# Where the halves of RWKV's token mixes are made: all of them on VectorE, stored split, and two LoRA products in float32

## The chip, the cores and the metric

One core of a Trainium2 chip runs the whole program. The metric is the device time of one launch in microseconds. The kernel before took 3241.56 us (median of three runs, 3240.18 to 3243.27). In the profile and below, PE is TensorE (PEld its weight loads), DVE is VectorE, ACT is ScalarE, POOL is GpSimd, and SP is SyncE, whose in-order queue issues nearly all DMAs.

## The reference

Two blocks follow one another on an activation of 256 tokens by 2048 features, in float32. The first block has four layers: an RWKV-7 mixer, a dilated attention, a pooling mixer, and again an RWKV-7 mixer. The second block has one attention with a linear recurrence and one mLSTM layer. The change touches only the front of the two RWKV mixers, which compute:

```
xx = shift(h) - h
r, k, v, g = [(h + xx * mu[j]) @ w_in[j] for j in 0..3]      # 2048 x 2048 each
xw, xa = h + xx * mu[4], h + xx * mu[5]
decay from tanh(xw @ w1) @ w2      (w1: 2048 x 96)
a     from (xa @ a1) @ a2          (a1: 2048 x 96)
v1, v2: the same kind of LoRA on the v mix, in the second RWKV layer only
```

After that come the recurrence over time (done in chunks of 64 tokens), a group norm, a gate with g, and the projection w_out (2048 x 2048).

## The kernel before

**Projections.** Every large product is made in three passes of the single-pass type float32r. Each operand is split into a high half (a cast, `split`, line 220, on ACT) and a low half (operand minus high half, line 221, on DVE), and TensorE adds high x high, high x low and low x high (line 262). `proj` runs over 512 columns of a weight at a time: over four chunks `c` of 512 input features and over two pairs of 128-row tiles, it loads 512 KB of weight into `wr` (3 buffers), splits it into `wh` and `wl` (5 buffers each, one k-tile each), and issues 6 matmuls per k-tile (3 passes for each of two token halves). The activation halves of a chunk are `ah` and `al`, four buffers each, so that one projection's input fills all of them.

**Order.** The code is written as generators (tasks) that a planner interleaves by estimated times; a scheduler then sets the final order of each engine's instructions when the program is built. Every engine works through its own list strictly in order.

**RWKV layer.** The mixes `h + xx*mu` are needed feature-major in chunks. `order` runs k, r, v for the first half of the columns and then again k, r, v for the second half, and the four column groups of g come last. So each mix is needed twice (g's only once, but late), and is kept in DRAM (`kept`, the `mix` tensors) in between:

- `first_mix` makes the k mix, chunk by chunk, at the layer's start; `mix` makes r and v while the projection before runs. The mix itself is one `scalar_tensor_tensor` on DVE per 128 features (line 485), then the split, then a DMA of the unsplit mix to DRAM (lines 517 and 498).
- `keep_g` makes the g mix by the slow way of `mixed`: a scaled copy on ACT (line 483) and an addition on POOL (line 487), and stores it unsplit (line 527).
- `again` reads a stored mix into an `st` buffer (2 buffers, 256 KB each, line 534) and splits it once more into `ah` and `al`.
- `lora` makes the w and a mixes by the slow way, casts the high half on ACT (line 576), subtracts on POOL (line 577), splits the LoRA weight into `z` buffers, and issues 12 float32r matmuls per chunk (`lora_mm`, lines 554 to 556).

**The blocks.** From the third projection on, `rwkv_blocks` runs eight blocks of the recurrence beside the projections: chains of small matmuls, DVE, ACT and POOL steps that carry high priority. From there until most of `w_out` is done, `lo_share = 3` sends every third weight's low half (line 221) to POOL in place of DVE.

Of the kernel before, what the change touches and what calls it, by code (L numbers as in the profile page):

```python
# [11 lines left out]
F32 = mybir.dt.float32  # L12
FR = mybir.dt.float32r
I32 = mybir.dt.int32
AF = mybir.ActivationFunctionType
OP = mybir.AluOpType
# [98 lines left out]
class Builder:  # L115
# [357 lines left out]
    def rwkv(self, ia, li):  # L473
# [4 lines left out]
        def mixed(m, j, c, a, slow=False):  # L478
            for f in range(2):
                ft = a * 2 + f  # L480
                mu = self.v("a_mu", ia * 6 + j, 16, c * 4 + ft)
                if slow:
                    nc.scalar.activation(m[:, f], st.xx[c][:, ft], AF.Copy, scale=mu)  # L483
                else:
                    ins = nc.vector.scalar_tensor_tensor(m[:, f], st.xx[c][:, ft], mu, st.h[c][:, ft], OP.mult, OP.add)  # L485
            if slow:
                ins = nc.gpsimd.tensor_tensor(m, m, st.h[c][:, a * 2:a * 2 + 2], OP.add)  # L487
            return ins

        kept = [self.dram.tile([128, 16, 256], F32, name="mix%d_%d" % (ia, j)) for j in range(4)]  # L490

        def mix(j, box, c):
            hi, lo = self.act_pair()
            for a in range(2):
# [3 lines left out]
                nc.sync.dma_start(kept[j][:, c * 4 + a * 2:c * 4 + a * 2 + 2], m)  # L498
# [3 lines left out]
        def first_mix(j, box):  # L502
# [5 lines left out]
            for u in range(8):  # L508
# [8 lines left out]
                nc.sync.dma_start(kept[j][:, c * 4 + a * 2:c * 4 + a * 2 + 2], m)  # L517
                if a:
                    box[c] = pair
                yield 0.6  # L520

        def keep_g():
            for c in range(4):
                for a in range(2):
                    m = self.t("st", [128, 2, 256], F32, 2)
                    mixed(m, 3, c, a, True)
                    nc.sync.dma_start(kept[3][:, c * 4 + a * 2:c * 4 + a * 2 + 2], m)
                    yield 3.0

        def again(j, box, c):  # L530
            hi, lo = self.act_pair()
            for a in range(2):
                m = self.t("st", [128, 2, 256], F32, 2)
                nc.sync.dma_start(m, kept[j][:, c * 4 + a * 2:c * 4 + a * 2 + 2])
                self.split(hi[:, a * 2:a * 2 + 2], lo[:, a * 2:a * 2 + 2], m)
# [31 lines left out]
        def lora(j, w1, n, tag, func):  # L567
            ws = lora_w(w1, n)
            q = self.gm()[0:n, 0:256]
            for c in range(4):  # L570
                hl = self.t("GM", [128, 2, 4, 256], FR, 3)
                for a in range(2):
                    m = self.t("e2", [128, 2, 256], F32, 7)
                    mixed(m, j, c, a, True)
                    s = slice(a * 2, a * 2 + 2)
                    nc.scalar.copy(hl[:, 0, s], m)
# [1281 lines left out]
```

## Time and profile before

| What | Value |
|---|---|
| median of three runs | 3241.56 us |
| profiled execution | 3250.24 us, with a span of 3247.1 us from first to last instruction |
| mean granted TensorE clock | 0.967 |
| PE, DVE, ACT, POOL busy | 93%, 71%, 55%, 24% of the span |
| HBM read and written | 527.88 MB and 46.15 MB, 177 GB/s over the span |

The profiled execution is 8.7 us longer than the median of the runs, and its span covers all but 3.1 us of it. The page gives busy shares over the whole span; the two RWKV layers fill about the first 800 us and the stretch from 1620 to 2410 us, and only there does the change move anything. A group's mean duration on DVE tells more than its busy time here, because the same instruction can take quite different times in different stretches.

### The profile page before, as it was taken

How to read it: one execution, taken by the hardware profiler on the slowest of the kernel's cores; microseconds unless marked ns; L12 is line 12 of the kernel's file. 1: busy time of each engine (PE TensorE's matmuls, PEld its weight loads, DVE VectorE, ACT ScalarE, POOL GpSimd, SP SyncE). 2: the span in 40 equal slices, each digit the busy share in tenths (PEclk: the TensorE clock that was granted, in tenths of full speed). 3: DMA queues.
4: the chain of work that ended last, by engine and by line, in shares of the span. 5: the costliest groups of instructions: out<-in, count | busy, mean ns of one | idle time of the engine just before them, and what ended most of it. 6: DMA issues, size and time to landing. Idle time of an engine off the chain costs nothing. (4 is left out here: it accounts for less than half of the span.)

```text
span 3247.1 us, 48857 instructions
## 1 busy us (share of the span) xinstructions
PE 3034.3 (93%) x17128; PEld 2452.2 (76%) x17128; DVE 2304.0 (71%) x4623; ACT 1783.2 (55%) x3504; POOL 794.6 (24%) x614
## 2 busy tenths in 40 slices
PE   6889999998999999999978898998989999999998
PEld 4667677776888888888856776777777788888886
DVE  7778778765666666676597788788557775666765
ACT  4565555444555555655555565554456765555554
POOL 4433443440112111020054325434312110000101
PEclk9999999999999999999989998999999999999999
DMA  5654453366666656666656644533665566666665
GB/s 186 200 193 145 155 175 121 122 200 203 178 174 178 177 169 205 205 211 191 208 174 219 197 152 153 171 119 105 206 214 160 156 188 203 182 199 172 186 187 169
DMA packets 327014, 577.24 MB, mean 178 GB/s; under 512 B 33856, under 2 KB 60776, under 8 KB 326768
## 3 DMA queue, kind: packets, MB, share of 16 engines
q1 hardware_dynamic: 326768, 574.12, 57.4%
q8 instruction: 134, 2.20, 0.3%
q14 instruction: 112, 0.92, 0.1%
HBM read 527.88 MB, written 46.15 MB: 177 GB/s over the span
## 5 line engine op out<-in xcount | busy, mean ns | idle before, releaser
L221 DVE TENSOR_TENSOR wl<-wr,wh 128x512 fp32r<-128x512 f32 x1580 | 1179.0, 758 | 690.8 <-ACT wh L220 664.3
L220 ACT CAST wh<-wr 128x512 fp32r<-128x512 f32 x1728 | 1052.4, 620 | 976.2 <-PE qps L262 452.9
L262 PE MATMUL qps<-wl,ah 128*128 128x512 f32 x3424 | 1385.8, 405 | 39.1 <-DVE wl L221 38.2
L262 PE MATMUL qps<-wh,al 128*128 128x512 f32 x3424 | 1368.7, 400 | 1.3 <-DVE al L221 1.3
L262 PE MATMUL qps<-wh,ah 128*128 128x512 f32 x3424 | 1266.3, 405 | 45.7 <-ACT wh L220 13.2
L262 PEld LDWEIGHTS qps<-wh,ah 128*128 128x128 f32 x3424 | 656.5, 192 | 191.0 <-ACT st L596 15.4
L262 PEld LDWEIGHTS qps<-wl,ah 128*128 128x128 f32 x3424 | 659.0, 192 | 187.2 <-DVE wl L221 53.3
L262 PEld LDWEIGHTS qps<-wh,al 128*128 128x128 f32 x3424 | 657.5, 192 | 137.9 <-DVE al L221 2.7
L221 POOL TENSOR_TENSOR wl<-wr,wh 128x512 fp32r<-128x512 f32 x148 | 203.6, 1385 | 363.9 <-ACT wh L220 336.3
L1103 POOL TENSOR_TENSOR q<-q,gain 128x1024 f32<-128x1024 f32 (+1 forms) x15 | 35.0, 2332 | 376.5 <-ACT sq L1097 376.5
L321 POOL TENSOR_TENSOR rstd<-rs_v,mhalf 128x2 f32<-128x2 f32 x7 | 5.0, 708 | 430.6 <-DVE rs_v L319 430.5
L277 PE MATMUL qtp<-cst,q 128*128 128x128 f32 x388 | 62.0, 289 | 23.0 <-DVE al L295 6.8
L838 PE MATMUL qtp<-q,q 64*128 64x128 f32 x512 | 72.4, 306 | 7.5 <-DVE GM L841 3.8
L277 PEld LDWEIGHTS qtp<-cst,q 128*128 128x128 f32 x388 | 48.5, 148 | 36.5 <-issue 20.5
L485 DVE SCALAR_TENSOR_TENSOR e<-q,vec,q 128x256 f32<-128x256 f32 x96 | 73.7, 811 | 0.0
L872 DVE TENSOR_TENSOR mb<-mb,Xc 128x120 f32<-128x120 f32 (+14 forms) x240 | 73.1, 305 | 0.1
L838 PEld LDWEIGHTS qtp<-q,q 64*128 64x128 f32 x512 | 57.9, 201 | 18.3 <-POOL q L811 5.1
L221 DVE TENSOR_TENSOR al<-st,ah 128x512 fp32r<-128x512 f32 x64 | 54.7, 871 | 23.5 <-ACT ah L220 23.4
L856 ACT COPY Md<-GM 32x128 f32<-32x128 f32 x128 | 55.3, 432 | 27.7 <-DVE GM L841 26.4
L220 ACT CAST ah<-st 128x512 fp32r<-128x512 f32 x64 | 38.3, 617 | 57.6 <-DMA st<-mix 49.7
L875 DVE TENSOR_TENSOR Xc<-Xc,mb 128x8 f32<-128x8 f32 x240 | 59.2, 247 | 1.1
L487 POOL TENSOR_TENSOR e<-e,q 128x512 f32<-128x512 f32 x32 | 48.2, 1521 | 31.8 <-ACT e L483 27.0
(388 smaller groups left out, 3383.2 us busy)
## 6 DMA issues: line engine op xcount, KB each, us to landing
wr<-a_w_in SPq DMA_DIRECT2D x256, 512.0 KB
wr<-b_w_in SPq DMA_DIRECT2D x160, 512.0 KB
wr<-odd_w_in SPq DMA_DIRECT2D x128, 512.0 KB
wr<-even_w_in SPq DMA_DIRECT2D x72, 512.0 KB
wr<-a_w_out SPq DMA_DIRECT2D x64, 512.0 KB
wr<-c_w_in SPq DMA_DIRECT2D x64, 512.0 KB
st<-mix SPq DMA_DIRECT2D x64, 256.0 KB
wr<-c_w_out SPq DMA_DIRECT2D x32, 512.0 KB
```

Of the source, the lines that this page charges most:

```text
L220: self.nc.scalar.copy(hi, src)
L221: (eng or self.nc.vector).tensor_tensor(lo, src, hi.bitcast(F32), OP.subtract)
L262: nc.tensor.matmul(o[:, cs], u[:, kk, sl], v[k][:, cs], start=st and x == 0 and c1 == 0, stop=sp and x == 2, skip_group_check=True)
L277: nc.tensor.transpose(q[:, f, t * 128:t * 128 + 128], src[:, t, (fp * 2 + f) * 128:(fp * 2 + f) * 128 + 128], self.ident)
L321: nc.gpsimd.tensor_tensor(r, v, self.mhalf[:, 0:2], OP.pow)
L485: ins = nc.vector.scalar_tensor_tensor(m[:, f], st.xx[c][:, ft], mu, st.h[c][:, ft], OP.mult, OP.add)
L487: ins = nc.gpsimd.tensor_tensor(m, m, st.h[c][:, a * 2:a * 2 + 2], OP.add)
L838: nc.tensor.matmul(qs[hp][:, c], BK[rs, f, c], AR[rs, f, c], start=True, stop=True)
L856: nc.scalar.copy(Md[rs, :, us].rearrange("p c u -> p u c"), GM2[rs, us, (1 - i // 2) ^ f, rs])
L872: nc.vector.tensor_tensor(mb[:, 0:n], mb[:, 0:n], Xc[:, r:r + 1].to_broadcast([128, n, 8]), OP.mult)
L875: nc.vector.tensor_tensor(Xc[:, r + 1], Xc[:, r + 1], mb[:, 0], OP.add)
L1103: nc.gpsimd.tensor_tensor(e3, e3, gain.unsqueeze(1).to_broadcast([128, 2 * nh, 128]), OP.mult)
```

## The change

All four stored mixes are stored as their two halves and read back straight into `ah` and `al`; the g mix and the two LoRA mixes are made by the DVE way; the first products of the w and a LoRAs run in float32 on the unsplit mix and the unsplit weight; and no low half is made on POOL any more. The v LoRA of the second RWKV layer keeps its split path.

```diff
-        def mixed(m, j, c, a, slow=False):
+        def mixed(m, j, c, a):
             for f in range(2):
...
-                if slow:
-                    nc.scalar.activation(m[:, f], st.xx[c][:, ft], AF.Copy, scale=mu)
-                else:
-                    ins = nc.vector.scalar_tensor_tensor(m[:, f], st.xx[c][:, ft], mu, st.h[c][:, ft], OP.mult, OP.add)
-            if slow:
-                ins = nc.gpsimd.tensor_tensor(m, m, st.h[c][:, a * 2:a * 2 + 2], OP.add)
+                ins = nc.vector.scalar_tensor_tensor(m[:, f], st.xx[c][:, ft], mu, st.h[c][:, ft], OP.mult, OP.add)
...
-        kept = [self.dram.tile([128, 16, 256], F32, name="mix%d_%d" % (ia, j)) for j in range(4)]
+        kept = [self.dram.tile([128, 4, 2, 4, 256], F32, name="mix%d_%d" % (ia, j)) for j in range(4)]
+
+        def keep(j, c, pair):
+            for i in range(2):
+                nc.sync.dma_start(kept[j][:, c, i], pair[i].bitcast(F32))
...
                 self.split(hi[:, a * 2:a * 2 + 2], lo[:, a * 2:a * 2 + 2], m)
-                nc.sync.dma_start(kept[j][:, c * 4 + a * 2:c * 4 + a * 2 + 2], m)
+            keep(j, c, (hi, lo))
...
                 self.split(pair[0][:, s], pair[1][:, s], m)
-                nc.sync.dma_start(kept[j][:, c * 4 + a * 2:c * 4 + a * 2 + 2], m)
                 if a:
+                    keep(j, c, pair)
                     box[c] = pair
...
         def keep_g():
             for c in range(4):
+                hl = self.t("GM", [128, 2, 4, 256], FR, 3)
                 for a in range(2):
-                    m = self.t("st", [128, 2, 256], F32, 2)
-                    mixed(m, 3, c, a, True)
-                    nc.sync.dma_start(kept[3][:, c * 4 + a * 2:c * 4 + a * 2 + 2], m)
+                    m = self.t("e2", [128, 2, 256], F32, 7)
+                    mixed(m, 3, c, a)
+                    s = slice(a * 2, a * 2 + 2)
+                    self.split(hl[:, 0, s], hl[:, 1, s], m)
                     yield 3.0
+                keep(3, c, (hl[:, 0], hl[:, 1]))
 
         def again(j, box, c):
             hi, lo = self.act_pair()
-            for a in range(2):
-                m = self.t("st", [128, 2, 256], F32, 2)
-                nc.sync.dma_start(m, kept[j][:, c * 4 + a * 2:c * 4 + a * 2 + 2])
-                self.split(hi[:, a * 2:a * 2 + 2], lo[:, a * 2:a * 2 + 2], m)
+            for i, d in enumerate((hi, lo)):
+                nc.sync.dma_start(d.bitcast(F32), kept[j][:, c, i])
...
         def lora(j, w1, n, tag, func):
-            ws = lora_w(w1, n)
+            w1 = w1.rearrange("(k p) n -> p k n", p=128)
+            ws = []
+            for a in range(2):
+                ws.append(self.t("z", [128, 8, n], F32, 4))
+                nc.sync.dma_start(ws[a], w1[:, a * 8:a * 8 + 8])
             q = self.gm()[0:n, 0:256]
             for c in range(4):
-                hl = self.t("GM", [128, 2, 4, 256], FR, 3)
+                ms = []
                 for a in range(2):
-                    m = self.t("e2", [128, 2, 256], F32, 7)
-                    mixed(m, j, c, a, True)
-                    s = slice(a * 2, a * 2 + 2)
-                    nc.scalar.copy(hl[:, 0, s], m)
-                    nc.gpsimd.tensor_tensor(hl[:, 1, s], m, hl[:, 0, s].bitcast(F32), OP.subtract)
+                    ms.append(self.t("e2", [128, 2, 256], F32, 7))
+                    mixed(ms[a], j, c, a)
                 yield 6.0
-                lora_mm(q, ws, c, hl[:, 0], hl[:, 1])
+                for f in range(4):
+                    nc.tensor.matmul(q, ws[c // 2][:, (c % 2) * 4 + f], ms[f // 2][:, f % 2], start=(c == 0 and f == 0),
+                                     stop=(c == 3 and f == 3))
+                self.pe(1.72)
             lora_fin(q, n, tag, func)
...
                     self.spawn(self.rwkv_blocks(ia))
-                    self.lo_share = 3
```

The order of instructions moves at many places of the two RWKV layers. Two places follow. The first is DVE's list in the start of the first RWKV layer, while the k projection begins; `e2` tiles are mixes, `wl` the weights' low halves, `al` the mixes' low halves, numbers are buffers. Before:

```order
L485 SCALAR_TENSOR_TENSOR e2_355<-q4_315,vec_97,q4_179 128x256 x2
L485 SCALAR_TENSOR_TENSOR e2_601<-q4_236,vec_97,q4_155 128x256 x2
L485 SCALAR_TENSOR_TENSOR e2_607<-q4_236,vec_97,q4_155 128x256 x2
L221 TENSOR_TENSOR wl_440<-wr_433,wh_439 128x512
L221 TENSOR_TENSOR al_348<-e2_349,ah_347 128x512
L221 TENSOR_TENSOR wl_458<-wr_455,wh_457 128x512
L221 TENSOR_TENSOR wl_462<-wr_455,wh_461 128x512
L221 TENSOR_TENSOR al_348<-e2_355,ah_347 128x512
```

The same place of DVE's list now:

```order
L482 SCALAR_TENSOR_TENSOR e2_354<-q4_315,vec_97,q4_179 128x256 x2
L482 SCALAR_TENSOR_TENSOR e2_531<-q4_236,vec_97,q4_155 128x256 x2
L482 SCALAR_TENSOR_TENSOR e2_534<-q4_236,vec_97,q4_155 128x256 x2
L482 SCALAR_TENSOR_TENSOR e2_583<-q4_236,vec_97,q4_155 128x256 x2
L482 SCALAR_TENSOR_TENSOR e2_588<-q4_236,vec_97,q4_155 128x256
L221 TENSOR_TENSOR wl_440<-wr_433,wh_439 128x512
L482 SCALAR_TENSOR_TENSOR e2_588<-q4_236,vec_97,q4_155 128x256
L221 TENSOR_TENSOR al_348<-e2_349,ah_347 128x512
L482 SCALAR_TENSOR_TENSOR e2_599<-q4_251,vec_97,q4_163 128x256 x2
L221 TENSOR_TENSOR wl_458<-wr_455,wh_457 128x512
```

Between the same two weight halves DVE now makes the w LoRA's mixes as well (`e2_531`, `e2_534`, `e2_599`). Counted up to the 48th `wl` of the list, there were 46 mix instructions, 16 low halves of mixes and 4 low halves of LoRA weights; now there are 90, 22 and none, and the g mix lies within that part.

The second place is SP's list at the first re-reading of the stored k mix (`mix0_1`), with the weight loads (`wr`) around it. Before:

```order
L225 DMA wr_1811<-a_w_in 128x2x512
L329 DMA kkb_3647<-a_rows 128x256
L534 DMA st_1722<-mix0_1_126 128x512
L683 DMA vt_1672<-v0_0_137 128x2x256
L683 DMA vt_2333<-v0_0_137 128x2x256
L534 DMA st_1726<-mix0_1_126 128x512
L225 DMA wr_1857<-a_w_in 128x2x512
L225 DMA wr_1904<-a_w_in 128x2x512
L534 DMA st_1829<-mix0_1_126 128x512
```

The same place of SP's list now:

```order
L225 DMA wr_1721<-a_w_in 128x2x512
L536 DMA ah_1596<-mix0_1_126 128x1024
L536 DMA al_1597<-mix0_1_126 128x1024
L225 DMA wr_1768<-a_w_in 128x2x512
L225 DMA wr_1817<-a_w_in 128x2x512
L225 DMA wr_1911<-a_w_in 128x2x512
L536 DMA ah_1697<-mix0_1_126 128x1024
L536 DMA al_1698<-mix0_1_126 128x1024
L225 DMA wr_1953<-a_w_in 128x2x512
```

Where loads of a half chunk into `st` stood, whole halves of a chunk go straight into `ah` and `al`, which come free only when TensorE has used the chunk before in that buffer; weight loads stand behind them in the same list.

## Rows read from the trace of the kernel before

**Rows 1.** The page, part 1: busy time of each engine

```profile
PE 3034.3 (93%) x17128; PEld 2452.2 (76%) x17128; DVE 2304.0 (71%) x4623; ACT 1783.2 (55%) x3504; POOL 794.6 (24%) x614
```

**Rows 2.** Busy time in five stretches (columns in the header line)

```profile
core 0: us, PE busy (x) PEld busy (x) DVE busy (x) ACT busy (x) POOL busy (x), PEclk, DMA share, GB/s
...
35.00:130.00 95.00, 75.66 (x312) 58.73 (x311) 91.31 (x103) 56.15 (x110) 56.29 (x40) 0.89 0.60 190
130.00:200.00 70.00, 64.51 (x309) 50.63 (x308) 49.33 (x85) 44.78 (x91) 22.63 (x18) 0.98 0.64 209
200.00:780.00 580.00, 533.24 (x4024) 418.85 (x4023) 440.65 (x1197) 303.71 (x666) 224.09 (x181) 0.94 0.51 161
1660.00:1760.00 100.00, 80.58 (x366) 64.55 (x367) 81.16 (x96) 58.44 (x115) 46.73 (x31) 0.93 0.64 205
1820.00:2400.00 580.00, 529.02 (x4026) 416.11 (x4025) 445.43 (x1242) 307.61 (x673) 227.79 (x179) 0.94 0.51 163
```

**Rows 3.** TensorE's waits, 35 to 130 us: total, times, longest

```profile
PE qps L262 <- DVE wl L221: 13.2, 9, 5.2
PE qgm L554 <- ACT z L220: 5.0, 1, 5.0
```

**Rows 4.** TensorE's waits, 1660 to 1760 us

```profile
PE qps L262 <- DVE wl L221: 10.5, 6, 5.7
PE qgm L554 <- ACT z L220: 3.7, 1, 3.7
```

**Rows 5.** Timeline 50 to 61 us: start, length, engine, line

```profile
52.42 6.53 DVE L485 SCALAR_TENSOR_TENSOR e<-q,vec,q 128x256 f32<-128x256 f32 x6
...
54.42 4.25 POOL L577 TENSOR_TENSOR GM<-e,GM 128x512 fp32r<-128x512 f32 x3
...
59.62 0.79 PE L262 MATMUL qps<-wl,ah 128*128 128x512 f32 x1 [5.25 <-DVE wl L221]
```

**Rows 6.** Groups by form, 35 to 130 us: busy us, mean ns

```profile
L221 DVE TENSOR_TENSOR wl<-wr,wh 128x512 fp32r<-128x512 f32 x38 | 37.9, 1025 | 2.5 <-ACT wh L220 2.5
...
L485 DVE SCALAR_TENSOR_TENSOR e<-q,vec,q 128x256 f32<-128x256 f32 x42 | 34.1, 853 | 0.0
...
L221 DVE TENSOR_TENSOR al<-e,ah 128x512 fp32r<-128x512 f32 x14 | 14.9, 1085 | 0.6 <-ACT ah L220 0.6
...
L221 DVE TENSOR_TENSOR z<-wr,z 128x768 fp32r<-128x768 f32 x4 | 6.0, 1490 | 0.0
L470 POOL TENSOR_TENSOR q<-q 128x510 f32<-128x510 f32 x4 | 5.2, 1302 | 5.3 <-PE qps L262 2.1 <-ACT ah L220 1.7 <-issue 1.4
...
L720 PE MATMUL qtp<-hw,lw 97*128 97x256 f32 x4 | 1.0, 378 | 0.0
```

**Rows 7.** The same view, 2650 to 3150 us, where GpSimd does little

```profile
L221 DVE TENSOR_TENSOR wl<-wr,wh 128x512 fp32r<-128x512 f32 x330 | 227.9, 697 | 151.3 <-ACT wh L220 147.2 <-PE qps L262 2.7
```

**Rows 8.** Line L485 alone: minimum, median, maximum in ns

```profile
L485 DVE SCALAR_TENSOR_TENSOR e<-q,vec,q x96: 467/474/1528, 29.1 to 1760.1; 128x256 f32<-128x256 f32 x96
```

**Rows 9.** Timeline of TensorE, 71 to 73 us

```profile
71.84 0.28 PE L554 MATMUL qgm<-GM,z 128*96 128x256 f32 x1
...
72.91 0.28 PE L554 MATMUL qgm<-GM,z 128*96 128x256 f32 x1
```

**Rows 10.** The page, part 5: groups of the whole span

```profile
L221 POOL TENSOR_TENSOR wl<-wr,wh 128x512 fp32r<-128x512 f32 x148 | 203.6, 1385 | 363.9 <-ACT wh L220 336.3
...
L221 DVE TENSOR_TENSOR al<-st,ah 128x512 fp32r<-128x512 f32 x64 | 54.7, 871 | 23.5 <-ACT ah L220 23.4
...
L220 ACT CAST ah<-st 128x512 fp32r<-128x512 f32 x64 | 38.3, 617 | 57.6 <-DMA st<-mix 49.7
```

**Rows 11.** Groups by form, 200 to 780 us

```profile
L221 DVE TENSOR_TENSOR wl<-wr,wh 128x512 fp32r<-128x512 f32 x166 | 134.0, 817 | 63.7 <-ACT wh L220 63.2
```

**Rows 12.** The page, part 6: DMA issues

```profile
st<-mix SPq DMA_DIRECT2D x64, 256.0 KB
```

**Rows 13.** Busy time in one short stretch

```profile
704.00:708.00 4.00, 4.00 (x27) 3.13 (x26) 0.72 (x3) 1.30 (x3) 0.00 (x0) 1.00 1.01 362
```

## The prediction

> **What bounds the kernel now.** I read the page's busy times first, then a table of stretches, then the waits of TensorE in the two stretches where it is least busy, then a timeline there, and last the groups by form, to see what one instruction costs in which company. TensorE is busy 93% of the span [rows 1], and the reader should look for the missing part: in the stretch 35 to 130 us, the start of the first RWKV layer, TensorE works 75.66 of 95 us while DVE works 91.31, so DVE is full there; in 1660 to 1760, the start of the second one, it is 80.58 and 81.16 of 100; in the long middles (200 to 780, 1820 to 2400) TensorE works 533 and 529 of 580 [rows 2]. In the starts TensorE waits for DVE's low halves of the weights, 13.2 and 10.5 us, and once for the LoRA weight's cast, 5.0 and 3.7 us [rows 3, 4]. The timeline shows how that arises: six mix instructions on DVE take 6.53 us where POOL runs its subtractions of the LoRA mixes, the next low half is late, and TensorE stands for 5.25 us [rows 5].
>
> What DVE pays there is mostly not its own work. A low half takes 1025 ns in the first start [rows 6] and 697 ns where POOL does little [rows 7]; a mix instruction 853 ns against a median of 474 over all [rows 6, 8]; a mix's low half 1085 ns [rows 6], a subtraction of the same shape as the weights'. The excess is 38 x 0.328 + 42 x 0.379 + 14 x 0.388 = 12.5 + 15.9 + 5.4 = 33.8 us of DVE's 91.31.
>
> **The starts.** POOL is busy 56.29 us in that stretch [rows 2]. The change takes away its mix additions and its subtractions; what stays is mainly the shifted differences of line 470, 5.2 us [rows 6], about a tenth. So I let nine tenths of the excess go: -30.7 us of DVE. The four low halves of LoRA weights go too: -6.0 us [rows 6]. Against that, up to the 48th low half of a weight in DVE's list there are now 44 more mix instructions and 6 more low halves of mixes (counted in the order): 44 x 0.474 + 6 x 0.697 = +20.9 + 4.2 us. The sum is -11.6 us, and since DVE stays the full engine (some 80 us of work), it is TensorE's time too. In the second start POOL is busy 46.73 us [rows 2]; scaled by that, 30.7 x 46.73/56.29 = 25.5, so -25.5 - 6.0 + 25.1 = -6.4. Both starts: -18 us. The ends: nothing, if the added mixes come at places where a weight's low half waits behind them (one such run of mixes in the order is longer now than before); and at best TensorE's idle time in the starts, 19.3 + 5.5 + 19.4 = 44 us [rows 2]. I take 18, the value that the durations give, nearer to the waits that would go first, the 8.7 us for LoRA casts [rows 3, 4], than to all of the idle time.
>
> By the Trainium skill ("SBUF — State Buffer", section "SBUF: two separate sides") the port that VectorE and GpSimd share is an exclusive lock: an instruction of VectorE with two SBUF inputs stands until GpSimd's instruction has ended, and the other way round. The trace agrees in kind (the 6.53 us beside POOL's 4.25). By the rule alone nearly all of POOL's removed 51 us would come off DVE, not 31; that is the first rival below, whose time is worked out from rows.
>
> **The LoRAs on TensorE.** Twelve float32r matmuls per chunk go, four float32 ones come. The old ones follow each other at 119 ns (nine steps in 1.07 us [rows 9]): 48 x 0.119 = 5.7 us per LoRA. A float32 product of 256 columns is shown by line L720: four records, two products, 1.0 us [rows 6], so 16 x 0.5 = 8.0 us. That is +2.3 us per LoRA, +9 us for four, in the starts, where TensorE waits a fifth of the time [rows 2]. I count +2; +9 if that cover goes.
>
> **The middles.** 148 low halves move from POOL [rows 10] to DVE: 148 x 0.697 = +103 us. The 64 second splits go: -54.7 us of DVE and -38.3 us of ACT [rows 10]. A low half on DVE costs 817 ns in the first middle [rows 11], 120 above the quiet value, over 166 of them 19.9 us; POOL's low halves are 101.8 of its 224 us there, so 45% of it goes, 9 us per layer, -18 us. DVE's net load is +30 us on 886 of 1160 us [rows 2], 76% to 79%. It also stops standing for the cast of a mix (23.5 us), and ACT stops standing for a stored mix's load (49.7 us) [rows 10]. DVE is nowhere full there, and TensorE's idle time, 46.8 + 51.0 us [rows 2], comes from chains in the blocks. I take 0. If TensorE's waits grow as DVE's free share shrinks, from 24 to 21%, it is 97.8 x (24/21 - 1) = +14; if a sixth of those waits goes with POOL's and ACT's delays, -15.
>
> **The queues.** A stored mix is now twice as large: 64 loads of 256 KB [rows 12] become 64 of 512 KB, and the writes likewise, +33.6 MB in all. In the first start 18 MB moved in 95 us at a share of 0.60 [rows 2], that is 317 GB/s at full share. With k, r and g stored in halves it is about 25 MB, 79 us of DMA time, just under DVE's 80 us of work. So hardly anything is left over; I count +1 us. On SP a re-read stands ahead of weight loads, and waits until TensorE has left the chunk whose buffers it fills. In the order, the four weight loads of the next two chunks stand before it. At 240 k-tiles in 580 us [rows 10, 11] a chunk of four lasts 9.7 us, so 19 us of weights are ahead, and a pair of halves lands in 1 MB / 362 GB/s = 2.9 us [rows 13]. I count 0.
>
> Sum: -18 + 2 + 0 + 1 = -15 us. From the profiled execution, 3250.2 us, that gives 3235; this execution was 8.7 us above the median of the runs, so the median goes from 3241.6 to about **3226 us**, with a range of its own of 3211 to 3234.
>
> **Rivals.** (1) POOL's removal gives more. TensorE becomes the bound in the starts; then its idle time there goes but for a few us, 44 - 4 = 40 us: 3202. For it: the single stall of 5.25 us begins with POOL [rows 5]; against it: DVE's added mixes stay. (2) What comes off DVE is eaten by what is put on it, in the starts by the longer run of mixes, in the middles by the 148 low halves: within 6 us of before, 3240. (3) The end on the other side: stored halves crowd the DMA engines. A chunk's pair is 512 KB longer than before, 1.65 us at 317 GB/s; there are 64 such pairs, 32 written and 32 read, 106 us. Hidden as long as weights are ahead; from 15/106, one in seven, laid open, the gain is gone, and with one in four it is -15 + 26 = +11: 3253. For it: the DMA share of 0.60 and 0.64 in the starts [rows 2] with 0.8 and more to come; against it: full rate is reached for 4 us at a time [rows 13] without TensorE stopping, and the middles are at 0.51 [rows 2]. (4) DVE's low halves make the blocks' chains late, +14 in the middles, with a start gain of only 5: 3251. (5) That the change does not do what it says is not open: in the order POOL holds no low half any more.
>
> **How the numbers follow.** My forecast gets 0.52, (1) 0.14, (2) 0.16, (3) 0.10, (4) 0.08. A measurement of this kernel tells 0.2%, 6.5 us, from no change. The forecast and (1) are faster: 0.66. (2), and nothing else, is the same: 0.16. (3) and (4) are slower: 0.18. The range of 8 in 10 leaves out a tenth at each side: 3196 to 3252, the lower end a little below (1), the upper one at (3) and (4).
>
> **What would show it.** In the first start: low halves of weights on DVE at about 720 ns in place of 1025, mix instructions near 500 in place of 853, DVE still busy over 90%, and TensorE's 5.0 us for the LoRA cast gone; POOL below 15 us there. In the middles: DVE at 78 to 80%, no idle time of ACT on a stored mix, and TensorE's idle time within 15 us of 98. The forecast is wrong if DVE's durations in the starts do not fall, if `wr` loads become what ACT waits for most in the starts, or if TensorE waits for a stored half (a matmul waiting for the load of `ah` or `al`) for more than a few us in all.

## The result, and the profile after

The changed kernel takes **3159.95 us** (median of four runs, 3156.79 to 3169.43), the kernel before on the same chip 3242.41: a ratio of **0.9749 (0.9731 to 0.9766)**, 82 us less where I had forecast 15. Measured once more later, it gave 0.9761 (0.9738 to 0.9784). The profiled execution below (3169.43 us, span 3167.6) is the slowest of its four.

The page's part 1, busy time of each engine over the span; it answers to [rows 1]:

```profile
PE 3017.3 (95%) x17064; PEld 2448.3 (77%) x17064; DVE 2247.9 (71%) x4811; ACT 1703.7 (54%) x3320; POOL 483.3 (15%) x386
```

The span is 79.5 us shorter, TensorE's busy time 17.0: so 62.5 us are waits of TensorE that went. Part of the 17.0 is TensorE's clock, which is higher in the starts' rows below; its products themselves got no cheaper by the change.

To see where, I cut every kernel's trace at the same places of the program: the casts of weights on ACT (`wh<-wr`), of which all kernels have 1728. Casts 1 to 81 are the start of the first RWKV layer, 81 to 305 its middle, 881 to 961 and 961 to 1169 those of the second one. A stage's idle time of TensorE is its length less TensorE's busy time. Busy time by these stages, first the kernel before (start, middle, start, middle; columns in the header), then the changed one, and as a fifth row the stretch that answers to the first of [rows 2]:

```profile
core 0: us, PE busy (x) PEld busy (x) DVE busy (x) ACT busy (x) POOL busy (x), PEclk, DMA share, GB/s
13.40:199.10 185.70, 147.94 (x640) 114.18 (x639) 154.20 (x210) 106.54 (x214) 83.04 (x63) 0.94 0.59 188
199.10:749.70 550.60, 510.26 (x3930) 400.77 (x3929) 425.30 (x1178) 290.24 (x637) 224.09 (x181) 0.95 0.50 158
1619.80:1804.60 184.80, 149.20 (x678) 118.15 (x676) 145.44 (x194) 104.84 (x205) 78.75 (x58) 0.93 0.61 195
1804.60:2340.40 535.80, 492.84 (x3889) 387.04 (x3889) 420.91 (x1207) 288.47 (x634) 221.40 (x175) 0.94 0.49 154
```

```profile
20.00:178.90 158.90, 143.41 (x634) 113.88 (x635) 138.41 (x279) 83.67 (x157) 22.94 (x25) 0.99 0.81 276
178.90:703.30 524.40, 498.44 (x3893) 393.93 (x3892) 398.55 (x1196) 272.80 (x596) 124.63 (x104) 0.95 0.55 180
1574.00:1733.60 159.60, 143.97 (x643) 114.65 (x642) 130.08 (x245) 79.91 (x146) 16.95 (x18) 0.95 0.79 268
1733.60:2256.00 522.40, 491.38 (x3895) 388.30 (x3894) 420.92 (x1244) 272.83 (x603) 130.89 (x107) 0.94 0.53 174
35.00:113.00 78.00, 76.08 (x321) 59.95 (x322) 76.23 (x148) 37.66 (x67) 8.66 (x10) 1.00 0.84 284
```

The starts are 26.8 and 25.2 us shorter (the first one begins 6.6 us later; SP now issues the loads of the LoRAs' second weights, `lw`, ahead of the first `wr`). The middles, which I had put at nothing, are **26.2 and 13.4 us** shorter. One place is not the same for TensorE: at the 81st cast it had issued 459 matmuls of projections before and 480 now. Cut at TensorE's own 480th and 1814th such matmul, the first middle is 21.6 us shorter (543.4 to 521.8) and the start, from the first of them to the 480th, 25.5; in the second layer such a cut alters the differences by 1 us or less. In the last row TensorE is busy 97.5% and DVE 97.7%: both are full, where before it was DVE alone.

TensorE's waits in that stretch (total, times, longest), against [rows 3]:

```profile
PE qps L262 <- DVE wl L221: 1.7, 3, 0.8
PE qps L262 <- DVE al L221: 0.6, 1, 0.6
```

Groups by form in the same stretch (count, then busy us and mean ns), against [rows 6]:

```profile
L482 DVE SCALAR_TENSOR_TENSOR e<-q,vec,q 128x256 f32<-128x256 f32 x82 | 36.5, 497 | 0.0
...
L221 DVE TENSOR_TENSOR wl<-wr,wh 128x512 fp32r<-128x512 f32 x40 | 26.9, 686 | 1.5 <-ACT wh L220 1.4
...
L582 PE MATMUL qgm<-e,z 128*96 128x256 f32 x64 | 15.8, 379 | 0.0
...
L221 DVE TENSOR_TENSOR al<-e,ah 128x512 fp32r<-128x512 f32 x15 | 12.4, 851 | 0.3 <-ACT ah L220 0.3
```

A mix takes 497 ns in place of 853, a weight's low half 686 in place of 1025. The LoRAs' float32 products (two LoRAs, 64 records) take 15.8 us, 7.9 each, as worked out.

Now the first middle. DVE's groups there (line, names, count, busy us and mean ns): a weight's low half, three operations of the blocks with both inputs in SBUF (`mb`, `Xc`, `S<-S`), and one that reads `qgy`, a PSUM tile. Before:

```profile
L221 DVE TENSOR_TENSOR wl<-wr,wh 128x512 fp32r<-128x512 f32 x150 | 123.4, 831 | 54.8 <-ACT wh L220 54.3
L872 DVE TENSOR_TENSOR mb<-mb,Xc 128x112 f32<-128x112 f32 (+14 forms) x119 | 38.4, 322 | 0.1
L875 DVE TENSOR_TENSOR Xc<-Xc,mb 128x8 f32<-128x8 f32 x120 | 29.6, 247 | 0.5
...
L1015 DVE TENSOR_TENSOR S<-S,fdb 128x256 f32<-128x256 f32 x16 | 10.6, 664 | 0.3
...
L1014 DVE TENSOR_TENSOR S<-qgy,S 128x256 f32<-128x256 f32 x16 | 6.7, 418 | 7.0 <-PE qgy L1004 6.9
```

and after:

```profile
L221 DVE TENSOR_TENSOR wl<-wr,wh 128x512 fp32r<-128x512 f32 x222 | 165.0, 752 | 74.0 <-ACT wh L220 73.2
L876 DVE TENSOR_TENSOR mb<-mb,Xc 128x88 f32<-128x88 f32 (+14 forms) x116 | 29.3, 253 | 0.1
...
L879 DVE TENSOR_TENSOR Xc<-Xc,mb 128x8 f32<-128x8 f32 x117 | 20.9, 179 | 0.5
...
L1019 DVE TENSOR_TENSOR S<-S,fdb 128x256 f32<-128x256 f32 x16 | 7.8, 484 | 0.2
L1018 DVE TENSOR_TENSOR S<-qgy,S 128x256 f32<-128x256 f32 x16 | 6.7, 416 | 0.7 <-PE qgy L1008 0.6
```

These three groups of the blocks became 21 to 28% shorter, the one that reads PSUM did not. Not every group with two inputs in SBUF gained as much: another `Xc<-Xc,mb` (L877, now L881) went from 220 to 211 ns.

### The profile page after: what moved, and what is told of

Its sections match the earlier page's. It is cut to its first block, busy times and chain, and to the rows that moved or that the text cites. A ratio compares the mean times of both kernels' runs of the same rounds, so it can differ in the third digit from the quotient of the medians.

```text
span 3167.6 us, 48383 instructions
## 1 busy us (share of the span) xinstructions
PE 3017.3 (95%) x17064; PEld 2448.3 (77%) x17064; DVE 2247.9 (71%) x4811; ACT 1703.7 (54%) x3320; POOL 483.3 (15%) x386
## 5 line engine op out<-in xcount | busy, mean ns | idle before, releaser
L221 DVE TENSOR_TENSOR wl<-wr,wh 128x512 fp32r<-128x512 f32 x1728 | 1243.8, 731 | 713.2 <-ACT wh L220 687.3
L482 DVE SCALAR_TENSOR_TENSOR e<-q,vec,q 128x256 f32<-128x256 f32 x192 | 86.6, 504 | 0.0
L1038 POOL TENSOR_TENSOR yt<-yt,gn_m 128x512 f32<-128x512 f32 x16 | 19.1, 1192 | 300.5 <-DVE gn_m L1037 191.6
L304 POOL TENSOR_TENSOR rk_y<-ss,mhalf 128x8 f32<-128x8 f32 x16 | 28.1, 1756 | 217.7 <-DVE ss L715 117.3
L876 DVE TENSOR_TENSOR mb<-mb,Xc 128x120 f32<-128x120 f32 (+14 forms) x240 | 59.8, 249 | 0.4
L845 DVE TENSOR_TENSOR GM<-qtp,cst 128x512 f32<-128x512 f32 x64 | 43.0, 684 | 18.7 <-PE qtp L842 16.7
L871 DVE STREAM_SHUFFLE mb<-Mc 128x120 f32<-128x120 f32 (+14 forms) x240 | 50.6, 223 | 0.1
L881 DVE TENSOR_TENSOR Xc<-Xc,mb 128x112 f32<-128x112 f32 (+6 forms) x224 | 47.6, 213 | 0.1
```

What stands on the lines that cost most here:

```text
L221: (eng or self.nc.vector).tensor_tensor(lo, src, hi.bitcast(F32), OP.subtract)
L845: nc.vector.tensor_tensor(GM[:, f * 2 + hp].rearrange("p (q a) n -> p q (a n)", a=2), qs[hp].rearrange("p (q a) n -> p q (a n)", a=2), gma ...
L871: nc.vector.stream_shuffle(mb[:, 0:15 - r], Mc[:, r + 1:16], [r] * 16 + [r + 16] * 16)
L876: nc.vector.tensor_tensor(mb[:, 0:n], mb[:, 0:n], Xc[:, r:r + 1].to_broadcast([128, n, 8]), OP.mult)
L881: nc.vector.tensor_tensor(Xc[:, r + 2:16], Xc[:, r + 2:16], mb[:, 1:n], OP.add)
```

## The experiments

**One part undone in the changed kernel.** First, every third low half on POOL again: `+ self.lo_share = 3` in the column loop.

> The changed kernel with one part undone: in the RWKV layers every third low half of a weight is made on GpSimd (POOL) again. Everything else, the stored halves too, stays as changed. Between before and after the middles of the RWKV layers became about 38 us shorter (24 and 13.5 us between the casts of the weights that bound them), which I had put at 0. Theory A (POOL's instructions lengthen DVE's beside them, in the blocks' chains too, and TensorE waits for these): the middles lose most of that again, 25 to 40 us, so 3185 to 3200 us; DVE's low halves of weights in the first middle go from about 730 back to about 800 ns, the blocks' multiplications from 249 back to about 300 ns. Theory B (the stored halves did it: ACT and DVE no longer stand in order for a mix that is read back): at most 8 us, 3155 to 3168. Theory C (the scheduler merely came to a luckier order): any sign, but without the durations of theory A.

3185.01 us, 0.9826 (0.98 to 0.9852): 25 us given back. The middles (first, second):

```profile
182.00:714.00 532.00, 496.49 (x3892) 390.40 (x3892) 385.02 (x1123) 272.20 (x597) 219.91 (x180) 0.96 0.55 177
1743.90:2282.80 538.90, 493.02 (x3891) 386.20 (x3891) 408.04 (x1174) 274.14 (x602) 216.14 (x175) 0.94 0.52 169
```

They are 7.6 and 16.5 us longer, although DVE has less to do. DVE's durations in the first one:

```profile
L221 DVE TENSOR_TENSOR wl<-wr,wh 128x512 fp32r<-128x512 f32 x149 | 119.3, 809 | 74.7 <-ACT wh L220 74.4
L877 DVE TENSOR_TENSOR mb<-mb,Xc 128x88 f32<-128x88 f32 (+14 forms) x116 | 35.2, 303 | 0.1
```

Theory A, durations included, with the time at its lower end. Second, unsplit stores:

```
- keep(j, c, (hi, lo))                       + nc.sync.dma_start(kept[j][..., 2 tiles], m)
- nc.sync.dma_start(d.bitcast(F32), ...)     + load m into st; self.split(hi, lo, m)
```

> The changed kernel with another part undone: the mixes are stored unsplit and split again by ACT and DVE after each re-read, as before; all mixes are made on DVE, no half on POOL, the LoRAs in float32. Theory A (POOL beside DVE): DVE gets 54.7 and ACT 38.3 us of splits back, in middles where neither is full, and no POOL work comes back: 0 to 10 us, 3160 to 3170. Theory B (standing for a stored mix): ACT's 49.7 and DVE's 23.5 us of standing return, and with them 25 us or more of the middles' gain: 3185 or more. In the starts k, r and v move half the bytes again, against some more splitting: within 5 us by both.

3168.89 us, 0.9774 (0.975 to 0.9799), 8 us more by the medians: in A's range, and B falls. It is not clear of the noise, as the changed kernel's second measurement is 0.9761 (0.9738 to 0.9784). The starts became 5.5 and 3.8 us shorter and the first middle 17.2 us longer, but in the first layer part of this is the cut: at the 81st cast TensorE had issued 459 matmuls of projections here, not 480. From its first to its 480th both kernels take the same time (150.0 and 150.5 us), and the middle from there on is 12.1 us longer. So only the second start, 3.8 us, speaks for a cost of the doubled bytes. TensorE's largest waits in the first middle:

```profile
PE qgm L899 <- DMA vt<-v: 7.4, 2, 6.9
PE qgy L993 <- DVE G L988: 6.3, 2, 5.8
PE qtp L784 <- DMA ld<-r: 5.4, 1, 5.4
```

Single stalls of 5 to 7 us, two of them for reloads of v and r. Third, the slow mixes:

```
- mixed(ms[a], j, c, a); mixed(m, 3, c, a)    + the same with slow=True (ACT scales, POOL adds)
```

> The changed kernel with a third part undone: the mixes of the two LoRAs of a start and of g are again a scaling on ACT and an addition on POOL. Low halves stay on DVE, the LoRAs in float32. The starts became about 52 us shorter in all (beside 6.6 us lost at the very first cast). Theory A (POOL's additions beside DVE cost the starts their time): DVE's mix instructions and low halves there rise towards 850 and 1000 ns, and the starts lose 20 to 30 us although DVE has 44 mix instructions fewer in each: 3180 to 3190. Theory D (the starts were short because DVE had less of its own work, without LoRA low halves and weights' low halves): taking 44 mixes of 0.47 us from DVE gains or changes nothing: 3145 to 3162.

3174.89 us, 0.9793 (0.9768 to 0.9817), 15 us more. Theory D falls. DVE's mixes and weights' low halves, 35 to 125 us, by form:

```profile
L221 DVE TENSOR_TENSOR wl<-wr,wh 128x512 fp32r<-128x512 f32 x42 | 35.2, 856 | 6.0 <-ACT wh L220 6.0
...
L485 DVE SCALAR_TENSOR_TENSOR e<-q,vec,q 128x256 f32<-128x256 f32 x37 | 27.7, 796 | 0.0
```

Half as many mixes as after, each 796 ns in place of 497; TensorE waits 8.3 us for low halves again; the starts are 9.9 and 8.2 us longer, 18 together, a little under the 20 to 30 that A expected. Fourth, float32r LoRAs, low halves on DVE:

```
- matmul(q, ws[..], ms[..])      + split mix (ACT, DVE) and weight; lora_mm(q, ws, c, hi, lo)
```

> The changed kernel with the LoRAs' first products on halves again, the low halves made on DVE (of the weights too), so POOL stays idle: TensorE has twelve float32r products of a chunk in place of four float32 ones, which I worked out as 2.3 us less for each LoRA, 9 us in all; DVE gets eight low halves of mixes (0.7 us) and four of weights (1.5 us) for each LoRA, some 11 us, twice in a start. Theory A1 (in the changed kernel TensorE is the full engine of the starts, 76.1 of 78 us, and DVE is no longer): 0 to -9 us, 3151 to 3160. Theory A2 (DVE still sets the starts): up to 22 us in a start, 3180 to 3200. The wait of TensorE for the cast of the LoRA weight (5.0 us before) returns in both, as a few us.

3168.96 us, 0.977 (0.9736 to 0.9805), 7 us more by the ratios, which alone is not clear of the noise: between A1 and A2. The first start ends 10 us later, the second is 8 us longer. TensorE's saving does not show.

**One part alone in the kernel before.** First, `- self.lo_share = 3`:

> The kernel before with one part of the change alone: no low half of a weight is made on GpSimd (POOL) any more; all else as before (mixes stored unsplit and split again, LoRA mixes and low halves with POOL). Theory A (POOL beside DVE costs the blocks' chains their time): undoing this part took 25 us from the changed kernel, so alone it gives 15 to 30 us here: 3210 to 3225, all of it in the two middles; DVE's multiplications of the blocks fall from 305 to about 260 ns, although DVE has 148 low halves (103 us) more. My forecast's step for the middles (nothing, between +14 and -15): 3225 to 3255. Theory C (luck of the order): any sign.

3207.05 us, 0.9897 (0.9877 to 0.9917): **34 us by this one line**, more than the 15 to 30 us that A expected. The middles:

```profile
197.00:715.70 518.70, 493.04 (x3925) 386.42 (x3924) 426.69 (x1249) 291.38 (x635) 128.64 (x107) 0.98 0.52 167
1766.70:2288.50 521.80, 490.43 (x3840) 386.95 (x3839) 430.45 (x1266) 288.41 (x627) 131.43 (x106) 0.95 0.49 158
```

31.9 and 14.0 us shorter, the starts hardly changed (183.9, 185.1), the stretch behind the second middle 10.9 longer. DVE's busy time rises by 1.4 and 9.5 us only, though it has 71 and 59 instructions more. In the first middle TensorE's idle time falls from 40.3 to 25.7 us; the other 17.2 us are its busy time, for as many matmuls (3930 and 3925): its granted clock is 0.98 there in place of 0.95. So over half of that stage's gain is TensorE's clock, which rose where TensorE stood less.

By which path POOL's halves cost time this run does not settle. TensorE itself waited for one of them only 0.8 us (its weight loads 2.0) in the whole trace of before. But a low half also frees its `wr` buffer, and SP's weight loads waited for those on POOL, in the first and the second middle of before:

```profile
SPq L225 <- POOL wl L221: 86.2, 27, 9.2
SPq L225 <- POOL wl L221: 97.2, 28, 11.7
```

Together with the waits for DVE's low halves (89.9 and 88.5 us) that is 176 and 186 us; with the one line less they are 137.0 and 135.8. This path goes with the line too, and no run tests it alone.

Second, stored halves:

```
kept as halves, again() loads them into ah, al; g mix: slow as before, then self.split
```

> The kernel before with the remaining part alone: all four mixes are stored as high and low halves and read back directly (the g mix still by ACT and POOL, then split by ACT and DVE); LoRAs in float32r with POOL's mixes and halves, every third low half of a weight on POOL. Theory B (ACT's 49.7 and DVE's 23.5 us of standing for a stored mix are worth time): the middles 15 us or more shorter: up to 3226. Theory A (these stands are hidden; putting the splits back cost the changed kernel 9 us, of which the middles hardly any but in the first one): 3228 to 3245; the starts get longer by up to 6 us, since twice the bytes are stored there.

3225.25 us, 0.9961 (0.9946 to 0.9975): 13 us, both middles 13 shorter (537.6, 522.6; the first one 8.7 when cut at TensorE's own matmuls). Theory B has a share. Third, the mixes alone:

```
- mixed(m, 3|j, c, a, True)      + mixed(m, 3|j, c, a)
- nc.gpsimd.tensor_tensor(low)   + nc.vector.tensor_tensor(low)
```

> The kernel before with another part alone: the mixes of the LoRAs and of g, and the LoRAs' low halves, are made on DVE in place of ACT and POOL; LoRAs still in float32r, mixes stored unsplit, every third low half of a weight still on POOL in the middles. Theory A: POOL is nearly idle in the starts, and DVE's instructions there fall to their quiet durations (mix near 500, weight's low half near 720 ns), but DVE gets all of the removed work: what the changed kernel gained in the starts without the float32 product, 10 and 16 us by the run with float32r LoRAs, so about 26 us less: 3210 to 3220. Rival (DVE is the full engine, so its added own work decides): 44 more mixes of 0.47 and 16 low halves of 0.7 us in each start eat the 30.7 and 25.5 us of relief: 3236 to 3246.

3238.65 us, 0.998 (0.996 to 1.0): theory A was wrong on the total, which lies in the rival's range, but right on the starts, 17.3 and 16.8 us shorter; the middles took it back, 23.0 and 5.5 longer:

```profile
13.10:181.50 168.40, 135.03 (x616) 106.05 (x615) 140.51 (x261) 84.80 (x157) 25.58 (x23) 0.99 0.66 212
181.50:755.10 573.60, 514.98 (x3953) 403.55 (x3952) 439.46 (x1188) 296.00 (x645) 232.06 (x181) 0.93 0.47 152
1623.90:1791.90 168.00, 146.14 (x670) 116.56 (x669) 137.88 (x258) 86.38 (x157) 17.14 (x18) 0.93 0.67 212
1791.90:2333.20 541.30, 486.92 (x3888) 383.07 (x3887) 425.76 (x1206) 288.17 (x634) 216.78 (x175) 0.95 0.48 153
```

DVE has 51 instructions more in the first start, and 13.7 us less busy time. First and third together:

> The kernel before with both parts together that went alone before: LoRA and g mixes with their low halves on DVE, and no low half of a weight on GpSimd (POOL). LoRAs in float32r, mixes stored unsplit. Alone the one gave 34 us (both middles 32 and 14 shorter), the other 2 us (both starts 17 shorter, but the first middle 23 and the second 5.5 longer). If they add: about 3205 us. If the second one's loss in the middles came from POOL's low halves beside DVE (theory A), it is gone here: starts 34 and middles about 39 shorter, 3165 to 3175, which leaves some 10 us for stored halves and float32 together.

3201.51 us, 0.9888 (0.9873 to 0.9903): they add (37). The stage picture of A was wrong: the middles stay at 542.6 and 540.1 though POOL is at 125 and 128 us, as in the changed kernel. So something else than POOL makes them long here.

**POOL's presence by itself.** The changed kernel with unused work:

```
+ if self.wcount % 3 == 0:   # for both k-tiles, in the RWKV layers
+     for i in range(3): nc.gpsimd.tensor_tensor(junk[:, 0:171], cst[171 columns], hi[k][:, 0:171], subtract)
```

> The changed kernel with unused work added on POOL in the RWKV layers: at every third weight tile, for each of its two k-tiles, three subtractions of 171 columns of SBUF data into a scratch of their own, that no other engine waits for; DVE's and ACT's work is as changed. That is about the POOL time which the removed low halves of weights took (some 100 us in each middle), without the low halves' own chain. Theory A1 (POOL's running beside DVE is what costs): the middles lose about what bringing back POOL's low halves cost, 15 to 30 us: 3175 to 3190, and DVE's low halves and block instructions lengthen as there. Theory A2 (it was the low half's own latency on POOL, 1.4 against 0.7 us, and POOL's queue in front of the blocks' POOL work): the dummies still stand in POOL's queue in front of the blocks' work, so a loss up to 10 us, with DVE's durations unchanged.

3204.27 us, 0.9886 (0.9869 to 0.9903): **44 us lost to work whose result nobody uses**. The middles, then the groups of DVE in the first of them and the dummies on POOL:

```profile
180.40:715.00 534.60, 498.97 (x3898) 391.00 (x3897) 439.31 (x1196) 273.21 (x595) 279.55 (x325) 0.96 0.55 177
1742.00:2292.00 550.00, 495.58 (x3875) 389.03 (x3874) 442.23 (x1240) 272.44 (x601) 269.47 (x311) 0.93 0.51 164
```

```profile
L223 DVE TENSOR_TENSOR wl<-wr,wh 128x512 fp32r<-128x512 f32 x223 | 187.7, 856 | 55.0 <-ACT wh L222 53.9
L883 DVE TENSOR_TENSOR mb<-mb,Xc 128x88 f32<-128x88 f32 (+14 forms) x116 | 34.0, 293 | 0.1
L886 DVE TENSOR_TENSOR Xc<-Xc,mb 128x8 f32<-128x8 f32 x117 | 27.6, 236 | 0.5
...
L1026 DVE TENSOR_TENSOR S<-S,fdb 128x256 f32<-128x256 f32 x16 | 9.9, 622 | 0.2
L1025 DVE TENSOR_TENSOR S<-qgy,S 128x256 f32<-128x256 f32 x16 | 6.7, 419 | 2.2 <-PE qgy L1015 2.0
...
L237 POOL TENSOR_TENSOR junk<-cst,wh 128x171 f32<-128x171 f32 x219 | 156.1, 713 | 132.4 <-ACT wh L222 121.1
```

The same 1196 instructions of DVE take 439.31 in place of 398.55 us, with 154.9 us more of POOL: 0.26 us for each. In the second middle it is 0.15: 21.3 us more of DVE (1240 instructions for 1244) for 138.6 of POOL. Low halves and the blocks' SBUF instructions lengthen, the one with a PSUM input stays at 419 ns. A1 holds in DVE's durations, and the time is beyond its 3190; A2, which had these durations unchanged, falls.

That all 44 us come by this path is not shown. The stages do not follow DVE's busy time: the first middle is 10.2 us longer where DVE has 41 more, the second 27.6 where it has 21 more. The order moved as well: 629 of DVE's 3804 instructions in the two layers do not lie in the longest order that its list shares with the changed kernel's. And the dummies read `wh`, whose buffer they hold, so that ACT's casts did wait for them, in the first and the second middle:

```profile
ACT wh L222 <- POOL junk L237: 4.3, 1, 4.3
ACT wh L222 <- POOL junk L237: 6.3, 3, 3.1
```

**The order by itself.** One number of the planner altered (`self.pe(1.72)` to `1.0`, or in the LoRAs with halves `self.pe(1.3)` to `0.58`), in five kernels:

> The changed kernel with one number of the planner altered: the time that it puts down for a LoRA chunk on TensorE is 1.0 in place of 1.72 us. No instruction is added or removed, only the order around it and after it moves. It sizes what order alone does here (theory C). Theory A: within 8 us of the changed kernel, 3152 to 3168, stage by stage too. Theory C: a middle that differs by 10 us or more at its end.

> The kernel before with one number of the planner altered (0.58 in place of 1.3 us put down for a LoRA chunk on TensorE): no instruction more or less, the order alone moves. Theory A (POOL beside DVE makes the middles long): within 10 us of the kernel before, its middles still 530 us or more each: 3230 to 3250. Theory C (the order decides): a middle of 520 us or less turns up, the time falls by 15 us or more.

> The kernel before without low halves of weights on POOL (3207 us, middles 519 and 522), with the planner's number altered. Theory A: its middles stay within 10 us of 520: 3197 to 3217. Theory C: one of them grows to 535 us or more: 3220 or more.

> The kernel before with no half of weights on POOL and the LoRA and g mixes on DVE (3201 us, middles 543 and 540, although POOL has as little there as in the changed kernel), with the planner's number altered. If unsplit stores with mixes on DVE make the middles long: 3195 to 3207, middles of 535 or more again. Theory C: at least one middle near 520, 3190 us or less.

> The changed kernel with unsplit stores (3169 us, middles 542 and 523), with the planner's number altered (1.0 in place of 1.72). If stored halves are worth the 17 us of the first middle: 3165 to 3175, first middle 535 or more. Theory C: first middle near 520, 3155 us or less, so that stored halves bring nothing.

| Kernel | ratio, altered | ratio, as it was | middles, altered | middles, as they were |
|---|---|---|---|---|
| changed | 0.9734 (0.9711-0.9757) | 0.9749 | 516.7, 513.1 | 524.4, 522.4 |
| before | 1.0015 (1.0002-1.0028) | 1 | 548.3, 537.1 | 550.6, 535.8 |
| no low halves on POOL | 0.9921 (0.9902-0.9941) | 0.9897 | 522.9, 524.2 | 518.7, 521.8 |
| and mixes on DVE | 0.9835 (0.9812-0.9857) | 0.9888 | 531.4, 536.4 | 542.6, 540.1 |
| changed, unsplit stores (order did not move) | 0.9768 (0.9751-0.9784) | 0.9774 | 540.9, 528.0 | 541.6, 522.7 |

How far the number moved DVE's list over the two layers (instructions outside that longest shared order): 123 of 3804 in the changed kernel, 353 of 3625 in the kernel before, 729 of 3757 without POOL's low halves, 536 of 3891 with the mixes on DVE as well, and none with unsplit stores. There every engine's list stayed as it was, so the last row is a second measurement of one program, and its question stays open.

The order moves a middle by up to 11 us and a kernel by up to 17. So theory C explains single differences of that size, not the 80 us. The middles of before stay long, those without POOL's low halves short. With mixes on DVE and unsplit stores (the last two rows) five of the six middles of three orders are above 530 though POOL does little; with stored halves all four of the changed kernel lie between 513 and 524. Stored halves added to the kernel of the fourth row make the one with float32r LoRAs (0.977), some 21 us from the faster of its two orders and 38 from the other. So the stored halves have a part in the gain beside the mixes on DVE, of a size that the order blurs.

**Less POOL still.** The blocks' two operand multiplications on DVE (`nc.gpsimd` to `nc.vector`), and then the group norm's and the keys' as well:

> The changed kernel with more taken from POOL: the two multiplications of each block's operands that POOL holds (about 1.0 us each for 128x256, 64 in all, 63 us) go to DVE, where the same shape takes 0.42 us: +27 us of DVE. By the run with unused POOL work (DVE 40.8 us longer for 155 us of POOL, 0.26 us for each) DVE gets 16 us back. Theory A with chains (each such pair shortens the chain in front of TensorE's operands by over 1 us): 0 to -10 us, 3150 to 3160. Rival (DVE's own work decides): 0 to +8.

> The changed kernel with nearly all of the blocks' POOL work on DVE: the operands' multiplications, the normalisation of a block's output (seven instructions of 128x512 and one of the keys, 1.1 to 1.7 us each on POOL, 0.68 on DVE). POOL loses some 217 us in two layers, DVE gets 104 and, at 0.26 us for each us of POOL, 56 back: net +48 us of DVE in two middles of 524, 81% in place of 76%. Theory A with chains (TensorE waits for chains, and these get shorter): -5 to -15 us, 3145 to 3155. Rival (a DVE over 80% busy lets the weights' low halves come late): 0 to +15 us.

3151.94 us, 0.9735 (0.9717 to 0.9752), and 3155.00 us, 0.974 (0.9723 to 0.9756). In the second POOL is down to 29.8 us in the first middle, which takes 517.1 us. The first one was run once more beside the changed kernel:

> The changed kernel itself once more, beside the version with the blocks' operand multiplications on DVE. By its first measurement 0.9749 of the kernel before (0.9731 to 0.9766), its middles 524 and 522 us in the profiled execution, which was the slowest of four; with the planner's number altered they were 517 and 513. Both theories: 3150 to 3168.

> The version with the blocks' operand multiplications on DVE once more, beside the changed kernel. Theory A with chains (TensorE still waits for chains that POOL holds up): 5 to 10 us below the changed kernel. Rival (once POOL holds neither weights' low halves nor mixes, what it still does costs TensorE nothing): within 4 us of the changed kernel, by 3155.

3164.04 (0.9761) and 3160.97 us (0.9741, 0.972 to 0.9762): not to be told apart. The rival holds; no version here is shown to beat the changed kernel.

## Why the prediction was wrong

The direction was right and the size five times too small: 15 us forecast, 82 measured, outside the range.

- **"The middles. ... I take 0": the step that failed.** They gave 39.6 us (34.7 at TensorE's own matmuls). What POOL's absence would take off DVE was priced from the weights' low halves alone, 9 us in each middle [rows 11]. By the busy times it was about 49 us in the first: DVE had 72 low halves more (72 x 0.69 = +50 us) and 32 splits less (32 x 0.87 = -28), and yet its busy time fell from 425.3 to 398.6. In the second (69 more, 32 less, no change) it was about 21. Of the 49, 18 are the low halves (222 of them, 79 ns each); most of the rest is the blocks' own instructions, which I left out. That the blocks' chains, and not DVE's share, set TensorE's idle time was written down ("comes from chains in the blocks") and then not priced: this idle time was to stay within 15 us of 98, and by the stages it fell from 83.3 to 57.0. The one-line kernel gives 34 us by what it takes from POOL (26 with the order altered), and unused work on POOL takes 44. That the way from DVE's instructions to TensorE leads through these chains is argued, not shown; the `wr` buffers and the order stand beside it. (A sixth of 97.8 us is 16, where I wrote 15.)
- **TensorE's clock: no term at all.** In the starts TensorE's busy time fell by 4.5 and 5.2 us, though the float32 products add 4.6 to each by my own sum. The granted clock went from 0.94 to 0.99 and from 0.93 to 0.95. By these shares TensorE lost 147.94 x 0.06 = 8.9 us and then 143.41 x 0.01 = 1.4 in the first start, 10.4 and then 7.2 in the second: an estimate of some 7 and 3 us that came back with the stalls gone.
- **DVE's share** was to go to 78 to 80%; it went from 77.2 to 76.0% in the first middle and from 78.6 to 80.6% in the second one.
- **The starts, -18: right in mechanism, too small.** All the signs came: 686 and 497 ns, DVE 97.7% busy, the LoRA cast's wait gone, POOL at 8.66 us. The failed part is that DVE's saving is TensorE's time: DVE's busy time fell by 15.8 and 15.4 us (forecast 11.6 and 6.4), the stages by 26.8 and 25.2, because TensorE's stalls for low halves went as well (13.2 to 1.7 us in the stretch above), the clock rose, and TensorE became as full as DVE. That is the first rival's picture of the starts, 40 us; its end, 3202, was still 42 us too high, for want of the middles. By itself the move of the mixes took 17 us from each start.
- **Rival 1's rule.** The lock of the shared port, as the Trainium skill has it ("SBUF — State Buffer", section "SBUF: two separate sides"), concerns VectorE's instructions with two SBUF inputs, and those in a mode that uses both ports. The rows agree on which instructions stand (`S<-S,fdb` 664, 484 and 622 ns, `S<-qgy,S` 418, 416 and 419); how long one does is not settled, since 154.9 us of POOL cost 40.8 us of DVE in one middle and 138.6 cost 21.3 in the other.
- **The LoRAs, +2.** TensorE's side was right (7.9 us for 8.0). The other side was missing: with halves on DVE the first start ends 10 us later and the second is 8 longer, as low halves of mixes and weights come back on a full engine; of the whole time 7 us, not clear of the noise.
- **The queues, +1.** With unsplit stores the second start is 3.8 us shorter, and the first one the same for the same matmuls, so the doubled bytes cost no more than a few us. The sign that `wr` loads lead ACT's waits came, 31.2 and 35.6 us in the two starts, but it told nothing: they led before as well, 29.7 and 29.1. No wait of TensorE for a stored half shows. Rival 3 did not come.
- **Rivals 2 and 4** expected DVE's added work to be paid in full. It was not: its instructions got shorter.

What stays open: the parts do not add. Alone they give 34, 13 and 2 us; the first and third together 37; with stored halves in float32r about 74, with float32 unsplit 73, with both 82. So either of the last two brings some 36 us, the second then 7 to 9, which is not clear of the noise. Float32 LoRAs alone on the kernel before were not run. Order accounts for up to 17 us of such differences: from the other order of the first and third together (0.9835) it is about 20 in place of 36. That unsplit loads put reloads of v and r late (waits of 6.9 and 5.4 us) fits the first middle, but was not tested by itself.

## What to carry to other kernels

Work moved to an engine that shares a resource can have a price on many instructions of the other engine, not only on the kind that was moved: compare the mean duration of all groups there with a quiet stretch, and above all of those in the chains that the bound engine waits for. Where two engines' lists are that full, price a change by the bound engine's waits in the stage, and what its clock does with them, not by the helper's busy time. Where order is set by a planner, run one kernel with the order shaken before reading meaning into 10 us, and compare the lists to see that it moved. Where stages are cut by one engine's instructions, count how far the others have come at the cut.

## What the runs showed of the hardware

- With 154.9 us more of POOL work on SBUF data, whose result nobody used, DVE's instructions with two SBUF inputs got longer: low halves 752 to 856 ns, `S<-S,fdb` 484 to 622 ns; one with an input in PSUM stayed at 416 to 419 ns. For each us of POOL it was 0.26 us of DVE in one middle, 0.15 in the other.
- Moving every third low half from POOL (1385 ns each) to DVE cost DVE 1.4 and 9.5 us of busy time in the two middles, where 130 instructions were added.
- The granted clock rose as TensorE's idle time went: in the first middle, with no low half on POOL, from 0.95 to 0.98 (a mean over stretches at the full level, 2.4 GHz, and the half one, 1.2), with idle time down from 40.3 to 25.7 us. 3930 matmuls took 510.26 us before and 3925 took 493.04.
